# Both FFNs of a decoder layer: gate and up products by Strassen's scheme over pairs of 272-token chunks, with the down products as a stage of their own

## The chip, the cores and the metric

The kernel runs on one core of a Trainium2 chip. The metric is the device time of one execution in microseconds (us). Engines are named as the profile names them: PE is TensorE's matmuls, PEld its weight loads, DVE VectorE, ACT ScalarE, POOL GpSimd, SP SyncE, whose queue issues all the transfers here.

## What is computed

One layer of a hybrid decoder, for 1024 prompt tokens and 64 sample tokens together (1088 columns), in float32:

```
x = x + 1/2 * SwiGLU_1(rmsnorm(x))
z = rmsnorm(x) @ w_in          # attention, recurrent branch, memory, gates
x = x + (sum_b gate_b * (y_b @ W_b_o)) @ w_out
x = x + 1/2 * SwiGLU_2(rmsnorm(x));  y = rmsnorm(x)
swiglu(x) = (silu(x @ w_gate) * (x @ w_up)) @ w_down
```

The model width is 1024 (8 row tiles of 128), the FFN width 2816 (22 tiles of 128, KF). Only the two SwiGLUs, what stands at their seams, and the preparation of weights change.

## The kernel before

Activations are feature-major: 128 features by tokens. The tokens are cut into three chunks of 352, 368 and 368 (CH). A product in float32 is done as three float32r matmuls of 128x128 weights by one chunk (mac3, lines 179 to 181): high weights by high data, high by low, low by high. Each matmul loads its weights anew. So every weight and every activation stands as two parts, a rounded high part that ACT copies and a low part that DVE subtracts.

Weights come by a plan (make_plan), in units of up to 128x1024: SP loads one into one of three raw buffers (line 141), ACT makes its high part (line 153) and DVE its low part (line 154), in one of four split buffers. ahead() makes the next unit while the current one is used.

In ffn() a gate tile and its up tile (144 matmuls: 2 products, 3 chunks, 8 row tiles, 3 matmuls each) are followed by evac: DVE multiplies gate by the reciprocal root-mean-square rbc (line 318), ACT applies Silu (319), DVE takes up times rbc and 1/2 (320), POOL multiplies (321), ACT and DVE split the result h (323, 324), which stays in SBUF. Between them stand the down products of the h tiles that are done: groups of 2, 2, 3, 3, 3, 3, 3 and 3 row tiles (DOWN), one PSUM bank per output tile and chunk, each added into x by DVE (line 348). In the last group, as each x tile becomes final, after() squares it on ACT (236), sums on POOL (238), and splits it for the next stage (198, 199).

```
[(0, 2, 512), (2, 2, 512)] + [(k, 3, 256) for k in range(4, 19, 3)] + [(19, 3, 1024)]
```

x stays in SBUF through an FFN. It is stored after FFN 1 (line 1333) and loaded again for the output projection (out_proj, line 1200), which adds to it, squares and splits it. The order on PE, ACT, DVE and POOL is that of the program's text, which tick() and later() interleave with side work (for instance bias_rows, lines 399 and 400, in FFN 1); SP issues in the program's order as buffers come free. PSUM has six banks for products and two for the rest.

## Time and profile before

| | us |
|---|---|
| runs of the kernel before | 2854.25, 2859.75, 2857.37 |
| median | 2857.37 |
| the profiled execution's own time | 2854.25 |
| its span, first to last instruction | 2854.3 |

The profile gives each engine's busy time over the span, by stretch, and by line. A matmul's own duration overlaps the next one's, so the cost of one in a full stream is the stretch's length over its number of matmuls. FFN 1 runs from 0 to about 818 us, the mixing part to about 1959, the output projection to about 2059, FFN 2 to 2839, and the final norm's tail to the end.

### The profile page before, as it was taken

The page shows a single profiled execution, that of the slowest core. Times are in us where ns is not written, and L with a number is a line of the kernel's source. Part 1 is how long each engine was busy: PE and PEld are TensorE (multiplying, and loading weights), DVE is VectorE, ACT ScalarE, POOL GpSimd, SP SyncE. Part 2 cuts the span into 40 slices and gives each one's busy share as a digit, 9 for nine tenths or more (in the row PEclk, how much of TensorE's full clock was granted, in tenths as well). Part 3 has the DMA queues.
Part 4 walks back from the last instruction along what each step waited for, and adds up shares of the span by engine and source line. Part 5 has one row for each costly group of instructions (what it writes and reads, how often), then busy time and mean ns, then how long its engine had stood idle before and what let it go on. Part 6 is the DMA issues. An engine that isn't in the chain of part 4 may idle for free. (4 is left out here: it accounts for less than half of the span.)

```text
span 2854.3 us, 40939 instructions
## 1 busy us (share of the span) xinstructions
PE 2801.9 (98%) x16762; PEld 2685.4 (94%) x16762; DVE 1309.6 (46%) x2204; ACT 748.5 (26%) x1306; POOL 449.0 (16%) x504
## 2 busy tenths in 40 slices
...
GB/s 155 78 96 72 84 76 62 84 77 62 77 167 120 97 128 71 186 194 183 169 154 147 120 79 56 255 189 191 89 74 74 67 78 78 67 78 78 67 74 63
DMA packets 142107, 308.03 MB, mean 108 GB/s; under 512 B 17800, under 2 KB 95816, under 8 KB 141248
## 3 DMA queue, kind: packets, MB, share of 16 engines
...
## 5 line engine op out<-in xcount | busy, mean ns | idle before, releaser
L179 PE MATMUL pg<-xg,ws 128*128 128x368 f32 (+1 forms) x2112 | 696.4, 330 | 6.1 <-ACT ws L153 6.1
L181 PE MATMUL pg<-xg,ws 128*128 128x368 f32 (+1 forms) x2112 | 694.4, 329 | 2.0 <-DVE ws L154 2.0
L180 PE MATMUL pg<-xg,ws 128*128 128x368 f32 (+1 forms) x2112 | 690.2, 327 | 0.5 <-DVE xg L199 0.5
L179 PE MATMUL z<-xg,ws 128*128 128x368 f32 (+1 forms) x1392 | 479.4, 344 | 6.0 <-DVE ta L1092 6.0
L181 PE MATMUL z<-xg,ws 128*128 128x368 f32 (+1 forms) x1392 | 457.0, 328 | 0.0
L180 PE MATMUL z<-xg,ws 128*128 128x368 f32 (+1 forms) x1392 | 456.1, 328 | 0.0
L154 DVE TENSOR_TENSOR ws<-wr,ws 128x1024 fp32r<-128x1024 f32 (+2 forms) x257 | 306.8, 1195 | 235.4 <-ACT ws L153 235.2
L179 PEld LDWEIGHTS pg<-xg,ws 128*128 128x128 f32 x2112 | 398.8, 189 | 6.4 <-ACT ws L153 6.1
L181 PEld LDWEIGHTS pg<-xg,ws 128*128 128x128 f32 x2112 | 398.9, 189 | 2.7 <-DVE ws L154 2.7
L180 PEld LDWEIGHTS pg<-xg,ws 128*128 128x128 f32 x2112 | 398.7, 189 | 2.4 <-DVE xg L199 2.4
L153 ACT ACTIVATE ws<-wr 128x1024 fp32r<-128x1024 f32 (+2 forms) x257 | 253.6, 989 | 543.6 <-PE pd L181 373.7
L180 PE MATMUL pd<-h,ws 128*128 128x368 f32 (+1 forms) x1056 | 346.2, 328 | 0.0
L179 PE MATMUL pd<-h,ws 128*128 128x368 f32 (+1 forms) x1056 | 346.0, 328 | 0.0
L181 PE MATMUL pd<-h,ws 128*128 128x368 f32 (+1 forms) x1056 | 345.5, 327 | 0.0
L321 POOL TENSOR_TENSOR td<-sl,tb 128x352 f32<-128x352 f32 (+1 forms) x132 | 128.4, 973 | 1336.7 <-DVE tb L320 1302.9
L179 PEld LDWEIGHTS z<-xg,ws 128*128 128x128 f32 x1392 | 263.2, 189 | 28.2 <-issue 19.0
L348 DVE TENSOR_TENSOR x<-x,pd 128x368 f32<-128x368 f32 (+1 forms) x384 | 199.0, 530 | 189.6 <-PE pd L181 189.5
L180 PEld LDWEIGHTS z<-xg,ws 128*128 128x128 f32 x1392 | 263.4, 189 | 2.8 <-issue 0.3
L181 PEld LDWEIGHTS z<-xg,ws 128*128 128x128 f32 x1392 | 262.8, 189 | 0.0
L320 DVE SCALAR_TENSOR_TENSOR tb<-pg,rbc 128x352 f32<-128x352 f32 (+1 forms) x132 | 70.7, 535 | 316.9 <-PE pg L181 316.9
L179 PEld LDWEIGHTS pd<-h,ws 128*128 128x128 f32 x1056 | 198.3, 188 | 0.0
L181 PEld LDWEIGHTS pd<-h,ws 128*128 128x128 f32 x1056 | 198.3, 188 | 0.0
...
## 6 DMA issues: line engine op xcount, KB each, us to landing
...
```

The source lines that it names most:

```text
L153: nc.scalar.activation(spl[:, 0, e], raw[:, e], AF.Copy)
L154: nc.vector.tensor_tensor(out=spl[:, 1, e], in0=raw[:, e], in1=spl[:, 0, e].bitcast(F32), op=OP.subtract)
L179: nc.tensor.matmul(out, wh, xh, start=i == 0, stop=False)
L180: nc.tensor.matmul(out, wh, xl, start=False, stop=False)
L181: nc.tensor.matmul(out, wl, xh, start=False, stop=i == n - 1)
L320: nc.vector.scalar_tensor_tensor(tb, pu[:, :n], 0.5, self.rbc[:, t0:t0 + n], op0=OP.mult, op1=OP.mult)
L321: nc.gpsimd.tensor_tensor(out=td, in0=sl, in1=tb, op=OP.mult)
L348: nc.vector.tensor_tensor(out=xa, in0=xa, in1=ps[:, :n], op=OP.add)
```

## The change

- Gate and up products of all 22 tiles come first, and the down products form a stage after them. h is stored to DRAM as it is made (line 491) and read back for the down stage (hidden, lines 548 to 553), where it is halved and split. The down groups become eleven of 2 row tiles.
- The tokens of gate and up are cut into two pairs (tp) of chunks of 272. Three tiles are done plainly (plain). The other 19 use Strassen's scheme in Winograd's form (quad): rows of weights in two halves, gate and up as the two halves of columns, two token chunks; seven products of 4 row tiles per pair where eight would stand, each with a combination of weights (combined, lines 172 to 205) and a combination of token blocks (token_blocks, sums_of_blocks). Three of the products add onto the banks of others, so a pair takes four banks, and the eight banks go to the two pairs.
- The tokens are scaled by the norm's gains, not by rbc, before they are split. rbc comes in at the evictions (swiglu, plain).
- The last two tiles (ALONE) are done for one token pair, then for the other, each with weights prepared anew, so that the first pair's memory is given to the down stage.
- Weights are split in halves of 512 in seven buffers (RING), with four raw buffers. The three lines of mac3 become 261 to 263.
- x is loaded again for each down stage, from the input in FFN 1, from DRAM in FFN 2 (line 1734). The output projection does chunks 2 and 1, then chunk 0; FFN 2 begins with the second token pair. The bias rows of FFN 1 come later and wait 20 ticks instead of 2.

**DVE in one tile of gate and up.** Before: the evacuation of one chunk (ta, tb, h: gate, up, the low part of h) and the split of a unit of weights (ws from wr). pg is a PSUM bank.

```order
L318 TENSOR_TENSOR ta_1271<-pg_1216,rbc 128x368
L320 SCALAR_TENSOR_TENSOR tb_1272<-pg_1241,rbc 128x368
L324 TENSOR_TENSOR h_1079<-td_1274,h_1079 128x368
L154 TENSOR_TENSOR ws_1301<-wr_1096,ws_1301 128x1024
```

Now, from a Strassen tile of FFN 1: ws is the low part of an operand, s and wr (L182) are the sums of weights, mu, uu and sl the sums of products of the two token pairs.

```order
L167 TENSOR_TENSOR ws_2908<-wr_2594,ws_2908 128x512
L182 TENSOR_TENSOR wr_2594<-wr_2594 128x512
L182 TENSOR_TENSOR s_2872<-wr_2594,wr_2592 128x512
L518 TENSOR_TENSOR uu_2914<-pg_2895,mu_2842 128x272
L518 TENSOR_TENSOR uu_2929<-pg_2916,mu_2857 128x272
L167 TENSOR_TENSOR ws_2944<-s_2872,ws_2944 128x512
L518 TENSOR_TENSOR uu_2914<-pg_2931,uu_2914 128x272
L518 TENSOR_TENSOR uu_2929<-pg_2948,uu_2929 128x272
L167 TENSOR_TENSOR ws_2974<-wr_2594,ws_2974 128x512
L533 TENSOR_TENSOR sl_2977<-pg_2826,rbc 128x272
L533 TENSOR_TENSOR sl_2991<-pg_2844,rbc 128x272
```

Between two operands' low parts there now stand two evacuations, which wait for PE's products of the operand before.

**SP where FFN 2 goes from gate and up to down.** Before, x was loaded once between the merge and the output projection, among the weights of w_out (xs_d is its copy in DRAM, wr a raw weight buffer):

```order
L141 DMA wr_17009<-in_w_out_dram 128x1024
L1200 DMA x_16988<-xs_d_86 128x8x368
L141 DMA wr_17041<-in_w_out_dram 128x1024
L1200 DMA x_16988<-xs_d_84 128x8x352
L141 DMA wr_17075<-in_w_out_dram 128x1024
```

Now it is loaded behind the last store of h (sl is h's buffer; hr a read of h):

```order
L491 DMA h_d<-sl_24824 128x544
L153 DMA wr_24940<-in_w_dn_dram 128x1024
L153 DMA wr_24978<-in_w_dn_dram 128x1024
L153 DMA wr_25034<-in_w_dn_dram 128x1024
L153 DMA wr_25138<-in_w_dn_dram 128x1024
L491 DMA h_d<-sl_24961 128x544
L1734 DMA x_25020<-x_d_82 128x8x352
L1734 DMA x_25020<-x_d_82 128x8x368 x2
L548 DMA hr_25229<-h_d 128x1088
```

The load of x moved from ahead of the output projection to behind the last gate and up tile of FFN 2, and it is in SBUF where that tile's buffers were.

The diff, cut to its core:

```diff
...
+TILES = [*range(KF), *range(KF - ALONE, KF)]
+DOWN = [(k, 2, 512) for k in range(0, KF - 2, 2)] + [(KF - 2, 2, 1024)]
+RING = 7
...
 UNITS = [(2, 0), (2, 1), (1, 0), (1, 1), (0, 0), (0, 1)]
-# tiles of the gates between the parts of the mixing layer: after the memory heads, after the attention heads,
...
...
-            pair = lambda p: [col(gu, p), col(gu, KF + p)]
-            plan, off = pair(0) + pair(1), 0
-            for g, (k, nk, w) in enumerate(DOWN):
-                if w == D:
-                    return plan + [flat(dn, off + j * 128 * D, D) for j in range(nk)]
-                k1, n1, _ = DOWN[g + 1]
-                plan += pair(k1) + [flat(dn, off + j * 128 * nk * w, nk * w) for j in range(D // w)]
-                plan += [u for p in range(k1 + 1, k1 + n1) for u in pair(p)]
+            plan, off = [], 0
+            for n, p in enumerate(TILES):
+                plan += [(gu if n < PLAIN else "*" + gu, i[gu][q], 1024) for q in (p, KF + p)]
+            for k, nk, w in DOWN:
+                n = D if w == D else nk * w
+                plan += [flat(dn, off + j * 128 * n, n) for j in range(nk * D // n)]
                 off += 128 * nk * D
+            return plan
...
-            spl = self.wspl.tile([128, 2, 1024], F32R, name=self.uid("ws"), tag="wspl")
-            for j in range(cuts):
-                e = slice(j * n // cuts, (j + 1) * n // cuts)
-                nc.scalar.activation(spl[:, 0, e], raw[:, e], AF.Copy)
-                nc.vector.tensor_tensor(out=spl[:, 1, e], in0=raw[:, e], in1=spl[:, 0, e].bitcast(F32), op=OP.subtract)
...
+    def part(self, src):
+        nc = self.nc
+        n = src.shape[1]
+        spl = self.wspl.tile([128, 2, 512], F32R, name=self.uid("ws"), tag="wspl")
+        nc.scalar.activation(spl[:, 0, :n], src, AF.Copy)
+        nc.vector.tensor_tensor(out=spl[:, 1, :n], in0=src, in1=spl[:, 0, :n].bitcast(F32), op=OP.subtract)
+        return spl
+    def halves(self, name, raw, n):
+        for a in range(0, n, 512):
+            self.ready.append((name, n, self.part(raw[:, a:min(a + 512, n)])))
+            yield
+    def combined(self, name, g, u):
+        nc = self.nc
+        a11, a12, a21, a22 = g[:, :512], g[:, 512:], u[:, :512], u[:, 512:]
+        s2 = self.sums.tile([128, 512], F32, name=self.uid("s2"), tag="s2", bufs=2)
+        def tt(eng, out, x, y, op):
+            eng.tensor_tensor(out=out, in0=x, in1=y, op=op)
+        def put(m, src):
...
+        put(4, a22)
+        tt(nc.vector, a22, a21, a22, OP.add)
+        tt(nc.vector, s2, a22, a11, OP.subtract)
+        tt(nc.gpsimd, a21, a11, a21, OP.subtract)
+        yield
+        put(6, s2)
+        yield
+        put(7, a21)
+        yield
+        put(5, a22)
+        yield
+        put(2, a12)
+        tt(nc.gpsimd, a12, a12, s2, OP.subtract)
+        yield
+        put(3, a12)
...
+    def make(self):
+        for _ in self.rest:
+            return
+        if self.raws or self.plan:
+            name, raw, n = self.raw()
+            if name[0] == "*":
+                self.rest = self.combined(name, raw, self.raw()[1])
+            else:
+                self.rest = self.halves(name, raw, n)
+            next(self.rest)
+            while len(self.raws) < 2 and self.plan:
+                self.load()
 
     def ahead(self):
-        if len(self.ready) + self.using < 4:
-            self.split()
+        for _ in range(2):
+            if len(self.ready) + self.using < RING:
+                self.make()
...
+    def operand(self, name, m):
+        while True:
+            for x in self.ready:
+                if x[:2] == (name, m):
+                    self.ready.remove(x)
+                    self.using += 1
...
-            nc.tensor.matmul(out, wl, xh, start=False, stop=i == n - 1)
+            nc.tensor.matmul(out, wh, xh, start=start and i == 0, stop=False, **more)
+            nc.tensor.matmul(out, wh, xl, start=False, stop=False, **more)
+            nc.tensor.matmul(out, wl, xh, start=False, stop=i == n - 1, **more)
             if i == min(3, n - 1):
                 self.ahead()
...
+        if gains is None:
+            nc.scalar.activation(t[:, 0], src, AF.Copy)
+            nc.vector.tensor_tensor(out=t[:, 1], in0=src, in1=t[:, 0].bitcast(F32), op=OP.subtract)
...
+        def squares(i, j):
+            src = self.block(xs, i, j)
+            for k in (0, 2):
+                t = pool.tile([128, 2, TC], F32, name=self.uid("sq"), tag="uu", bufs=3)
+                nc.scalar.activation(t, src[:, k:k + 2], AF.Square)
+                for e in range(2):
+                    if j not in acc:
+                        acc[j] = pool.tile([128, TC], F32, name=self.uid("acc"), tag="mu", bufs=2)
+                        nc.gpsimd.tensor_tensor(out=acc[j], in0=t[:, 0], in1=t[:, 1], op=OP.add)
+                        break
+                    nc.gpsimd.tensor_tensor(out=acc[j], in0=acc[j], in1=t[:, e], op=OP.add)
...
+            squares(i, j)
+            for k in range(4):
+                nc.scalar.activation(src[:, k], src[:, k], AF.Copy, scale=self.vec[:, g + 4 * i + k:g + 4 * i + k + 1])
+            if not (quick and n < 2):
+                self.put(tp, m, src)
+            if (1 - i, j) in order[:n]:
+                self.later(3, lambda j=j: rstd(j))
+            yield
...
+        b11, b12, b21, b22 = (self.block(xs, i, j) for i in range(2) for j in range(2))
+        def less(out, x, y):
+            eng.tensor_tensor(out=out, in0=x, in1=y, op=OP.subtract)
+        less(b11, b12, b11)
+        less(b12, b22, b12)
+        less(b22, b22, b11)
+        yield
+        self.put(tp, 6, b22)
+        yield
+        self.put(tp, 7, b12)
+        less(b21, b21, b22)
+        yield
+        while not rest():
+            yield
+        self.put(tp, 5, b11)
+        yield
+        self.put(tp, 4, b21)
+        yield
...
+                for w in ws:
+                    while not all(m in xo for m in ms):
+                        self.tick()
+                    ps = self.mm_bank("pg")
+                    self.mac3(ps[:, :TC], [(w(k, 0), (xo[ms[k // 4]][:, 0, k % 4, :], xo[ms[k // 4]][:, 1, k % 4, :]))
+                                           for k in range(KD)])
+                    both.append(ps)
...
+                def evac(j=j, rb=rb, both=both, sl=sl, uu=uu, tp=tp):
+                    for t, ps in zip((sl, uu), both):
+                        nc.vector.tensor_tensor(out=t[:, j], in0=ps[:, :TC], in1=rb, op=OP.mult)
+                    if j:
+                        self.gated_hidden(p, tp, sl, uu)
+                self.held.append(((tp, j), evac))
+                self.evacuate(2)
+        for _ in ws:
+            self.done()
...
+    def gated_hidden(self, p, tp, sl, uu):
+        nc = self.nc
+        nc.scalar.activation(sl, sl, AF.Silu)
+        nc.gpsimd.tensor_tensor(out=sl, in0=sl, in1=uu, op=OP.mult)
+        nc.sync.dma_start(self.h_d[p, :, tp * TH:(tp + 1) * TH], sl.rearrange("p j n -> p (j n)"))
+    def quad(self, gu, p, tps, pool):
+        banks, steps = {}, {tp: self.swiglu(p, tp, pool) for tp in tps}
+        for m in OPS:
+            w = self.operand("*" + gu, m)
+            for tp in tps:
+                bank = {2: 1, 4: 7, 3: 5}.get(m, m)
+                if bank == m:
+                    banks[tp, m] = self.mm_bank("pg")
+                ps, xo = banks[tp, bank][:, :TC], self.xo[tp][m]
+                self.mac3(ps, [(tuple(w[:, s, k * 128:(k + 1) * 128] for s in range(2)), (xo[:, 0, k, :], xo[:, 1, k, :]))
+                               for k in range(4)], start=bank == m)
+                steps[tp](m, ps)
+            self.using -= 1
...
+        def step(m, ps):
+            if m == 1:
+                new("mu", [TC], 2)
+                nc.scalar.activation(t["mu"], ps, AF.Copy)
+            if m == 6:
+                plus(t["mu"], ps, t["mu"])
+            if m == 7:
+                new("uu", [2, TC], 3)
+                plus(t["uu"][:, 1], ps, t["mu"])
+            if m == 5:
+                plus(t["uu"][:, 1], ps, t["uu"][:, 1])
+            if m == 2:
+                new("sl", [2, TC], 3)
+                nc.vector.tensor_tensor(out=t["sl"][:, 0], in0=ps, in1=rb[:, 0], op=OP.mult)
+            if m == 4:
+                plus(t["uu"][:, 0], ps, t["mu"])
+                nc.gpsimd.tensor_tensor(out=t["uu"], in0=t["uu"], in1=rb, op=OP.mult)
+            if m == 3:
+                sl = t["sl"]
+                plus(sl[:, 1], ps, t["mu"])
+                nc.gpsimd.tensor_tensor(out=sl[:, 1], in0=sl[:, 1], in1=rb[:, 1], op=OP.mult)
+                self.gated_hidden(p, tp, sl, t["uu"])
+        return step
+    def hidden(self, k, pool, raws, wait):
+        nc = self.nc
+        raw = raws()
+        nc.sync.dma_start(raw, self.h_d[k])
+        def split():
+            h = pool.tile([128, 2, NT], F32R, name=self.uid("h"), tag="h", bufs=4)
+            nc.scalar.activation(h[:, 0, :], raw, AF.Copy, scale=0.5)
+            nc.vector.scalar_tensor_tensor(h[:, 1, :], raw, 0.5, h[:, 0, :].bitcast(F32), op0=OP.mult, op1=OP.subtract)
+            self.h[k] = h
+        self.later(wait, split)
...
+        second = 1 - first
+        for p in range(PLAIN):
+            self.copies(copies)
+            self.plain(gu, p, (first, second), pool)
+        self.evacuate(0)
+        self.plained = True
+        while self.first or self.due:
+            self.tick()
+        self.hurry = False
+        for p in range(PLAIN, KF - ALONE):
+            self.copies(copies)
+            misc(p)
+            self.quad(gu, p, (first, second), pool)
+        for tp in (first, second):
+            for p in range(KF - ALONE, KF):
+                self.quad(gu, p, (tp,), pool)
+            if tp == first:
+                change()
...
+    def down(self, dn, pool, raws, after):
+        for g, (k, nk, w) in enumerate(DOWN):
+            ks = range(k, k + nk)
+            if 0 < g < len(DOWN) - 1:
+                for j in range(2):
+                    self.hidden(DOWN[g + 1][0] + j, pool, raws, 8 + 4 * j)
+            if w == D:
+                units = [self.unit(dn, w) for _ in ks]
                 for c in range(3):
-                    evac(p, c, *[product(w, c, 2) for w in ws])
-
-        def down_tile(ks, part, o, c):
-            t0, n = CH[c]
-            ps = self.mm_bank("pd")
-            self.mac3(ps[:, :n], [(part(j), tuple(h[k][:, s, t0:t0 + n] for s in range(2))) for j, k in enumerate(ks)])
-            xa = self.x[:, o, t0:t0 + n]
-            nc.vector.tensor_tensor(out=xa, in0=xa, in1=ps[:, :n], op=OP.add)
-            self.tick()
-
...
             nc.sync.dma_start(self.bias_d[g], row)
             for h in range(4):
...
+        nc = self.nc
+        for tp in (1, 0):
+            nc.sync.dma_start(xs[tp], self.x_d[0][:, :, tp * TH:(tp + 1) * TH])
+        for cs in ((2, 1), (0,)):
...
+                            xa = xs[tp][:, f, a - tp * TH:e - tp * TH]
+                            nc.vector.tensor_tensor(out=xa, in0=xa, in1=ps[:, a - t0:e - t0], op=OP.add)
+                    self.tick()
                 self.done()
-                if 0 in cs:
-                    split(2, f)
-                    if f == 2:
-                        self.norm_chunk(2, accs[2], 2)
-        for c in range(2):
-            for f in range(KD):
-                split(c, f)
-            self.later(2 + c, lambda c=c: self.norm_chunk(c, accs[c], 3))
-
...
+    def change2():
+        low2.close()
+        pools.append(right(low2, "ring2"))
+        four = stage0.tile([128, 4, NT], F32, name="hr4", tag="xs")
+        raws = iter([four[:, k] for k in range(4)])
+        K.first_hidden(pools[-1], lambda: next(raws), lambda: None)
...
-        K.ring = es.enter_context(tc.tile_pool(name="ring2", bufs=4, reuse_waits="tile"))
-        K.tmps = es.enter_context(tc.tile_pool(name="tmps4", bufs=2, reuse_waits="tile"))
+        K.banks(es, "psum6", mm=6, t=2)
...
-        K.out_proj(pool)
+        for t0, n in CH:
+            nc.sync.dma_start(K.x[:, :, t0:t0 + n], K.x_d[1][:, :, t0:t0 + n])
         acc = {}
...
-        K.ffn("w_gu2", "w_dn2", (2, 0, 1), lambda c: None, after2, lambda p: K.copies(1 if p < 21 else 100))
+        K.down("w_dn2", ring, K.raw_tiles(pool), after2)
...
```

## Rows read from the trace of the kernel before

**Rows 1.** The page, part 1: span and busy time by engine.
```profile
span 2854.3 us, 40939 instructions
...
PE 2801.9 (98%) x16762; PEld 2685.4 (94%) x16762; DVE 1309.6 (46%) x2204; ACT 748.5 (26%) x1306; POOL 449.0 (16%) x504
```
**Rows 2.** Busy time by stretch (us, then busy and instructions by engine, clock, DMA share, GB/s): steady FFN.
```profile
2200.00:2300.00 100.00, 100.00 (x609) 100.00 (x608) 38.25 (x65) 16.48 (x27) 8.76 (x9) 1.00 0.22 74
```
**Rows 3.** The page, part 5: one of the gate and up products' three lines.
```profile
L179 PE MATMUL pg<-xg,ws 128*128 128x368 f32 (+1 forms) x2112 | 696.4, 330 | 6.1 <-ACT ws L153 6.1
```
**Rows 4.** Timeline of PE, memory keys (256 columns): the first product, and what follows the last of 96.
```profile
853.15 0.28 PE L179 MATMUL mk<-mg,ws 128*128 128x256 f32 x1
...
864.55 0.39 PE L833 MATMUL mv<-ws,mg 128*128 128x512 f32 x1
864.78 0.39 PE L834 MATMUL mv<-ws,mg 128*128 128x512 f32 x1
```
**Rows 5.** Busy time by stretch: the start, and the bias rows at 140.
```profile
0.00:10.00 10.00, 2.79 (x7) 1.88 (x7) 5.18 (x7) 6.44 (x12) 5.61 (x10) 1.00 0.80 274
10.00:20.00 10.00, 8.61 (x33) 6.90 (x34) 10.00 (x10) 8.84 (x18) 9.69 (x9) 1.00 1.05 393
20.00:30.00 10.00, 10.00 (x65) 10.00 (x64) 10.00 (x16) 6.15 (x13) 1.63 (x2) 1.00 0.16 62
30.00:40.00 10.00, 7.27 (x37) 6.76 (x36) 8.23 (x21) 3.62 (x8) 2.42 (x2) 0.83 0.37 117
140.00:150.00 10.00, 7.16 (x45) 6.87 (x43) 2.52 (x4) 1.97 (x3) 0.98 (x1) 1.00 0.23 75
150.00:160.00 10.00, 9.28 (x44) 8.50 (x45) 2.71 (x6) 1.00 (x2) 0.95 (x1) 0.83 0.60 187
```
**Rows 6.** Groups by form (busy us, mean ns, then idle before): splits and evacuations.
```profile
L154 DVE TENSOR_TENSOR ws<-wr,ws 128x1024 fp32r<-128x1024 f32 x183 | 230.1, 1258 | 180.9 <-ACT ws L153 180.7
L153 ACT ACTIVATE ws<-wr 128x1024 fp32r<-128x1024 f32 x183 | 192.4, 1052 | 481.9 <-PE pd L181 373.7 <-PE pg L181 54.3 <-PE z L181 34.4
L348 DVE TENSOR_TENSOR x<-x,pd 128x368 f32<-128x368 f32 x256 | 135.4, 536 | 145.0 <-PE pd L181 145.0
L321 POOL TENSOR_TENSOR td<-sl,tb 128x368 f32<-128x368 f32 x88 | 86.6, 984 | 600.3 <-DVE tb L320 580.6 <-ACT sl L319 19.5
L690 POOL TENSOR_TENSOR qb<-qb,kv 128x1024 f32<-128x1024 f32 x24 | 57.6, 2398 | 235.1 <-DMA qb<-qs_d 151.9 <-DVE s L510 23.8 <-DVE st L538 16.6
L318 DVE TENSOR_TENSOR ta<-pg,rbc 128x368 f32<-128x368 f32 x88 | 47.3, 537 | 49.3 <-PE pg L181 49.2
L319 ACT ACTIVATE sl<-ta 128x368 f32<-128x368 f32 x88 | 45.1, 512 | 175.5 <-DVE ta L318 175.5
```
**Rows 7.** Instructions of tile mg and of L199 (ns min/median/max, first and last start).
```profile
L800 DVE SCALAR_TENSOR_TENSOR mg<-mraw,vec,mg x8: 477/482/486, 824.7 to 836.3; 128x256 fp32r<-128x256 f32 x8
...
L199 DVE SCALAR_TENSOR_TENSOR xg<-x,vec,xg x72: 576/597/1408, 5.1 to 2062.6; 128x368 fp32r<-128x368 f32 x48, 128x352 fp32r<-128x352 f32 x24
```
**Rows 8.** Timelines at the end of FFN 1: POOL, then DVE.
```profile
785.29 8.20 POOL L238 TENSOR_TENSOR acc<-acc,td 128x352 f32<-128x352 f32 x7 [5.14 <-ACT td L236]
...
787.05 0.84 DVE L199 SCALAR_TENSOR_TENSOR xg<-x,vec,xg 128x352 fp32r<-128x352 f32 x1
...
788.24 0.84 DVE L199 SCALAR_TENSOR_TENSOR xg<-x,vec,xg 128x352 fp32r<-128x352 f32 x1
```
**Rows 9.** Timelines of SP and DVE: x is loaded again before the output projection.
```profile
1959.84 0.59 SPq L1200 DMA_DIRECT2D x<-xs_d  x1
1966.61 0.54 DVE L1216 TENSOR_TENSOR x<-x,wo 128x368 f32<-128x368 f32 x1 [5.21 <-DMA x<-xs_d]
```
**Rows 10.** Busy time by stretch: that load; and the tail.
```profile
1965.00:1970.00 5.00, 5.00 (x32) 5.00 (x31) 1.86 (x3) 1.46 (x2) 0.00 (x0) 1.00 1.05 404
2840.00:2854.30 14.30, 2.35 (x15) 1.86 (x15) 7.55 (x13) 0.93 (x2) 4.57 (x5) 0.57 0.51 185
```
**Rows 11.** Timeline of the tail: the last output stores.
```profile
2846.65 3.83 SPq L1239 DMA_DIRECT2D out_y_dram<-x  x4
```

401 lines of the change are left out of this document (245 added, 156 removed).

## The prediction

> **What bounds the kernel now.** The page's busy times come first: TensorE is busy 98% of 2854.3 us, VectorE 46%, GpSimd 16% [rows 1]. So only the number and length of matmuls, or new waits of TensorE, can move the time. The stretches of both FFNs come next: 609 matmuls in 100 us at full clock, with DVE at 38%, ACT 16%, POOL 9% and the DMA at 0.22 [rows 2]. That is 0.1642 us each at a mean of 1088/3 = 362.7 columns; nothing there waits. Each of the three lines of the gate and up products has 2112 matmuls, 6336 together [rows 3], 1040 us of the span. The other rows give prices for what the change puts in.
>
> The profiled execution took 2854.25 us; the median of the runs is 2857.37, so 3.1 us go on top of a sum made against it. A measurement of this kernel can tell some 0.2%, 5.7 us, from no change.
>
> **The gate and up products.** Per FFN three plain tiles keep 576 matmuls (2 products x 4 blocks x 24). The other 19 take 7 products x 2 token pairs x 12 = 168 each, 3192, where the three chunks had 19 x 144. Both FFNs: 7536 matmuls of 272 columns. No row has 272. The nearest are 256 columns, where 96 matmuls take 853.15 to 864.55, 0.1188 each [rows 4], and 0.1642 at 362.7 [rows 2]. These bound the whole at 895 and 1237 us. The line between them gives 0.000426 us per column; carried to 512 it gives 0.228, and the row there shows 0.23 (864.55 to 864.78), so I take the line: 0.1256. The stage takes 946.5 us instead of 1040.4: **-94**. A tile takes 21.1 us instead of 23.6.
>
> **What the other engines do in a Strassen tile** (the first order extract). VectorE has 9 operations of 512 elements with both inputs in SBUF (seven low parts, two sums of weights) and 12 of 272 from PSUM. By rows of 256 (0.48) [rows 7] and 1024 (1.26) [rows 6] one of 512 takes 0.74; by L318 (0.54 at 368) one of 272 takes 0.43: 6.7 + 5.2 = 11.9 us of 21.1. GpSimd has two of 512 at 1.29, four of 544 at 1.36 and two of 272 at 0.78, between L321 and L690 [rows 6]: 9.6. ACT has seven copies at 0.63, two of 272 and two Silus of 544: 6.6. Two h stores and later one read add 1.1 MB per tile to DMAs at 0.22. What can lengthen this is the two engines meeting: where POOL ran seven sums back to back at 1.17, DVE's L199 took 0.84 against 0.58 free, and one pair of operations came every 1.19 us (787.05 to 788.24) [rows 7, 8]. Free, the pair is 0.58 + 0.95 = 1.53, so it overlaps in part; the factor is 0.78. Even at that, 5.2 + 0.78 x (6.7 + 9.6) = 17.9 is under 21.1: **0**, hidden by TensorE, with 3 us of room. Seven operands of lookahead (10 us of TensorE) cover the order of the queues. If the cover is gone, the tile becomes VectorE's (below).
>
> The Trainium skill speaks against this: on the page "SBUF — State Buffer", section "Who interferes with whom", a VectorE instruction with two SBUF inputs and a GpSimd instruction that reads SBUF exclude each other for the whole instruction. By it the pair above would take 1.53, and the row shows 1.19, so the trace bears out a contention but not a whole exclusion. By it VectorE's time in a tile would be 21.5 and the term about +15 instead of 0.
>
> **Last two tiles, one token pair at a time.** Each pass has 84 matmuls, 10.55 us, and still all nine VectorE operations on weights: 6.7 + 2.6 = 9.3 alone, GpSimd 6.1, met as above 2.6 + 0.78 x 12.8 = 12.6. Eight passes, each short of 2.0 us at most, with 10 us of operands ahead at each row of four; copies of h to be read (1088 elements, 1.3 us) come on top. From 0 to 16, I take **+4**, since the lookahead covers most.
>
> **Start.** Before, 142 matmuls ran in the first 40 us, worth 23.3, so 16.7 were lost [rows 5]; and 89 ran in 140 to 160 (14.6 of 20), 5.4 lost to the bias rows, which the change puts off by 20 ticks. Now ACT prepares eight blocks of 272 tokens: two squares of 544 at 0.66, four scalings at 0.43, one copy of 1088 at 1.1, 4.1 us a block by L319 and L153 [rows 6]. With seven weight halves the first token pair is ready near 25 us and the second near 45, while TensorE has some 18 us of work: about 27 lost. 27 - 16.7 - 5.4 = 5: **+6** (0 if the blocks come as fast as chunks did; 14 if GpSimd's sums hold them).
>
> **End of FFN 1.** The last down group has 2 row tiles instead of 3, so TensorE needs 6 x 0.1642 = 0.99 us per output tile, and VectorE's pair 1.19 [rows 8]: 24 x 0.20 = **+5** (2 with free pairs, 12 at L199's 1.41). The other ten groups are safe: 24 additions at 0.53, four halves and two reads of h are 18 us of 23.6. **Mixing:** split weights come in halves, 0.22 us more VectorE time for each of 129 units, and 3.5 units ahead instead of 4; nearly all is beside TensorE: **+1** (-4 by the fourth raw buffer, +10 if a third of the 28 us counts).
>
> **Output projection to FFN 2.** The blocks are squared, scaled, copied and combined by the same ACT that splits weights; only chunks 2 and 1's 16 tiles and then chunk 0's pass (8 x 24 x 0.16 = 31 us) lie beside eight blocks, 33 us: **+5** (1 to 13).
>
> **FFN 2, gate and up to down** (second extract). x no longer stays in SBUF. Its load lies on SP behind the last h store, and its memory is that of the tile stored. After TensorE's last product: addition 0.43, product 0.78, Silu 0.66, product 1.36, then the store's landing. At the end of the program the last store (issued by 2850.5) lands by 2854.3 [rows 10, 11]: below 4 us for a larger piece; I take 3. x takes 6.8 us from issue to first use (1959.84 to 1966.61) [rows 9] and its other two chunks 3.6 us each (1.47 MB at 404 GB/s) [rows 10]. First addition 13 us after the last product, third chunk 20. Six PSUM banks take 6 tiles, the first two chunks let 8 finish: 7.9 us of work. 20.2 - 7.9 = 12.3, and a lower clock after it, as at 30 to 40 us (0.83) [rows 5], makes **+14**. Bounds: 7, if landing is quick and chunks come together; 20, if the h reads crowd in. FFN 1 reads x from the input in time: 0. **Tail:** the last group is shorter by a third with the same final norm: **+2** (0 to 6).
>
> **Sum.** -94 + 6 + 0 + 4 + 5 + 1 + 5 + 14 + 2 = -57: 2797 against the profiled execution, **2800** against the median.
>
> **Rivals.**
> 1. The stalls are mostly hidden: all terms at their low ends, 0 + 0 + 0 + 2 - 4 + 1 + 7 + 0 = 6: 2769. For it: each has some cover; against it: the first FFN already loses 22 us in its start with less to prepare [rows 5].
> 2. Whole exclusion of VectorE and GpSimd, as worked out from the rows' free durations: a tile is 5.2 + 16.3 = 21.5, 38 x 0.4 = +15; a single pass 2.6 + 12.8 = 15.4, 4.9 over, 39 in eight less two lookaheads of 10: +19 instead of +4. 2830. Against it: 1.19 where it wants 1.53 [rows 8]. This is the rule named above.
> 3. Slower: the lookahead collapses. VectorE's queue is in order, and between the low parts stand evacuations that wait for TensorE (first extract). If an operand's low part is behind the evacuations of the product before it, TensorE waits 2 x 0.43 + 0.74 = 1.6 us. Once in each of 38 tiles costs 61, twice 122: 2861 and 2922. It decides from 1.5 us a tile. For it: in the first 20 us DVE is busy 10 of 10 us with ten operations [rows 5], 1.0 us each. Against it: seven operands are far more than one.
> 4. No gain, because a matmul of 272 columns costs what one of 363 does: 1237 instead of 1040, slower by 140 or more. The 0.1188 of rows 4 all but excludes it.
>
> **How the numbers follow.** The forecast, 2783 to 2820, has a chance of 0.60; the stalls bigger together than summed, 2820 to 2840, 0.10; rival 1 0.16; rival 2 0.07; rivals 3 and 4 0.06 and 0.01. The range 2768 to 2832 leaves out part of the third case and rivals 3 and 4, and takes in the bounds by halves. Faster by over 0.2% (below 2851.7) 0.91, the same 0.02, slower 0.07.
>
> **What would show it.** Right: about 795 matmuls per 100 us in the Strassen tiles (0.1256), PE near 100%, DVE near 60%, POOL 45%; some 25 us of PE idle in the first 50; one PE wait of about 12 us for x after FFN 2's last gate tile, its releaser DVE behind a DMA. Wrong: PE waits for ws in every tile (rival 3), DVE operations of 512 near 1.4 us mean (rival 2), or no wait for x.

## The result, and the profile after

The changed kernel takes 2874.19 us (median of 4 runs, 2873.31 to 2875.31) where the kernel before took 2858.56 in the same series: ratio 1.0051, 95% interval 1.0037 to 1.0065. It is slower, by 15.6 us; 2800 with a range of 2768 to 2832 was forecast. The profiled execution has a span of 2871.6 us, 17.3 more than before. One run of the study, e4_xrows, had a granted clock of 0.76 from start to end and took 3303.75 us; it is not used, and e4b_xrows repeats it.

The page of the changed kernel, its first part and two of its groups (busy us, mean ns, idle before):

```profile
span 2871.6 us, 45875 instructions
...
PE 2745.8 (96%) x17980; PEld 2620.9 (91%) x17980; DVE 1699.0 (59%) x2961; ACT 889.3 (31%) x1673; POOL 780.1 (27%) x726
...
L261 PE MATMUL pg<-xo,ws 128*128 128x272 f32 x2512 | 736.2, 293 | 46.9 <-DVE uu L518 18.9 <-ACT xo L372 10.8 <-ACT ws L166 9.4
...
L167 DVE TENSOR_TENSOR ws<-wr,ws 128x512 fp32r<-128x512 f32 x592 | 477.4, 832 | 317.3 <-ACT ws L166 316.7
```

TensorE's matmuls are busy 56 us less than before [rows 1]; the gate and up products wait 46.9 us in one of their three lines where they waited 6.1 [rows 3]. Busy time by stretch (us, then busy and instructions by engine, clock, DMA share, GB/s):

```profile
0.00:50.00 50.00, 30.37 (x181) 28.36 (x181) 17.86 (x32) 38.64 (x72) 27.26 (x34) 0.86 0.46 175
...
200.00:250.00 50.00, 44.63 (x335) 43.59 (x334) 25.83 (x44) 11.75 (x22) 19.67 (x16) 0.93 0.36 129
...
350.00:400.00 50.00, 50.00 (x401) 50.00 (x401) 30.52 (x54) 13.98 (x26) 22.41 (x18) 1.00 0.35 128
...
500.00:550.00 50.00, 43.62 (x300) 42.13 (x298) 32.30 (x53) 20.10 (x34) 22.18 (x17) 0.91 0.72 257
...
2050.00:2100.00 50.00, 46.42 (x326) 45.89 (x327) 26.81 (x46) 27.11 (x44) 24.67 (x20) 0.97 0.61 208
...
2200.00:2250.00 50.00, 50.00 (x403) 50.00 (x402) 31.55 (x53) 15.48 (x30) 23.37 (x19) 1.00 0.57 196
...
2550.00:2600.00 50.00, 33.67 (x194) 31.49 (x194) 25.01 (x42) 11.44 (x19) 8.92 (x7) 0.83 0.53 186
```

A full stretch of Strassen tiles (350, 2200) holds 402 matmuls, 0.1244 us each, at full clock and with VectorE at 61%: the promise of the products is kept. The rest is lost in a few places, and in each the granted clock falls after the wait: 0.83 to 0.97 are means over 50 us, partly at 2.4 and partly at 1.2 GHz. In what follows, a tile's *lost* time is the time from its first matmul to the next tile's, less 0.1244 us for each of its matmuls (0.1642 for down tiles). By stage, after less before:

| stage | forecast | measured |
|---|---|---|
| gate and up products themselves | -94 | -97 |
| FFN 1 start (before: 21.3 lost to 60 us) | +11 | +13 |
| bias rows (before: 7.8 lost at 120 to 160; after: 23.3 in four tiles) | -5 | +15 |
| eight passes of one token pair | +4 | +29 |
| FFN 1, gate and up to down (2.6 lost), and its last group (2.0 lost before, 7.5 after) | +5 | +8 |
| mixing and merge (1140.7 before, 1152.0 after) | +1 | +11 |
| projection (95.8 before, 102.8 after), start of FFN 2 (2.0 lost before, 13.7 after) | +5 | +19 |
| FFN 2, gate and up to down (17.6 lost), and 0.33 us a down group | +14 | +21 |
| last group of FFN 2 (2.1 lost before, 5.8 after) and tail (15.6 before, 18.4 after) | +2 | +7 |
| sum | -57 | +26 |

The measured rows sum to 26 where the span grew by 17.3. Most of the difference is small losses that the kernel before had elsewhere and that are gone: 4.1 us between 160 and 780, 2.0 between 2080 and 2780. Three rows (bias rows, passes, projection with the start of FFN 2) hold 59 of the 83 us by which the rows missed.

### The profile page after: what moved, and what is told of

Read it like the earlier page. It is cut to its first block, busy times and chain, and to the rows that moved or that the text cites. A ratio compares the mean times of both kernels' runs of the same rounds, so it can differ in the third digit from the quotient of the medians.

```text
span 2871.6 us, 45875 instructions
## 1 busy us (share of the span) xinstructions
PE 2745.8 (96%) x17980; PEld 2620.9 (91%) x17980; DVE 1699.0 (59%) x2961; ACT 889.3 (31%) x1673; POOL 780.1 (27%) x726
## 4 chain that ended last, share of the span: by engine, by line
PE 76%; DVE 7%; DMA 6%; POOL 4%; ACT 3%; issue 3%; SPq 0%; DVEq 0%; ACTq 0%; POOLq 0%
PE pg L261 7%; PE pg L263 7%; PE pg L262 7%; PE z L261 7%; PE z L262 6%; PE z L263 6%; PE pd L261 6%; PE pd L262 6%; PE pd L263 6%; DMA wr<-in_w_gu_dram 2%; PE po L263 2%; PE po L262 2%; PE t L1005 2%; PE po L261 2%; DMA out_sv_dram<-in_cache_v_dram 2%
## 5 line engine op out<-in xcount | busy, mean ns | idle before, releaser
L261 PE MATMUL pg<-xo,ws 128*128 128x272 f32 x2512 | 736.2, 293 | 46.9 <-DVE uu L518 18.9
L263 PE MATMUL pg<-xo,ws 128*128 128x272 f32 x2512 | 731.6, 291 | 4.1 <-DVE ws L167 4.1
L262 PE MATMUL pg<-xo,ws 128*128 128x272 f32 x2512 | 732.4, 292 | 2.7 <-DVE xo L373 2.6
L167 DVE TENSOR_TENSOR ws<-wr,ws 128x512 fp32r<-128x512 f32 x592 | 477.4, 832 | 317.3 <-ACT ws L166 316.7
L166 ACT ACTIVATE ws<-wr 128x512 fp32r<-128x512 f32 x592 | 346.0, 613 | 765.1 <-PE pd L263 392.8
L261 PEld LDWEIGHTS pg<-xo,ws 128*128 128x128 f32 x2512 | 481.5, 192 | 52.1 <-DVE uu L518 21.6
L263 PEld LDWEIGHTS pg<-xo,ws 128*128 128x128 f32 x2512 | 481.6, 192 | 4.8 <-DVE ws L167 4.8
L262 PEld LDWEIGHTS pg<-xo,ws 128*128 128x128 f32 x2512 | 481.8, 192 | 3.8 <-DVE xo L373 3.3
L620 DVE TENSOR_TENSOR x<-x,pd 128x352 f32<-128x352 f32 (+1 forms) x528 | 270.6, 529 | 163.7 <-PE pd L263 148.7
L261 PEld LDWEIGHTS z<-xg,ws 128*128 128x128 f32 x1392 | 263.7, 189 | 28.7 <-issue 19.1
L261 PEld LDWEIGHTS pd<-h,ws 128*128 128x128 f32 x1056 | 200.2, 190 | 16.6 <-DVE x L620 16.0
L262 PEld LDWEIGHTS pd<-h,ws 128*128 128x128 f32 x1056 | 200.6, 190 | 0.0
L263 PEld LDWEIGHTS pd<-h,ws 128*128 128x128 f32 x1056 | 200.5, 190 | 0.0
L320 POOL TENSOR_TENSOR acc<-acc,td 128x368 f32<-128x368 f32 (+1 forms) x41 | 43.2, 1054 | 496.7 <-ACT td L318 494.6
```

The costliest lines, as they stand in the source:

```text
L166: nc.scalar.activation(spl[:, 0, :n], src, AF.Copy)
L167: nc.vector.tensor_tensor(out=spl[:, 1, :n], in0=src, in1=spl[:, 0, :n].bitcast(F32), op=OP.subtract)
L261: nc.tensor.matmul(out, wh, xh, start=start and i == 0, stop=False, **more)
L262: nc.tensor.matmul(out, wh, xl, start=False, stop=False, **more)
L263: nc.tensor.matmul(out, wl, xh, start=False, stop=i == n - 1, **more)
L320: eng.tensor_tensor(out=acc[:, :n], in0=acc[:, :n], in1=t, op=OP.add)
```

## The experiments

Each edit is against the changed kernel, with nothing else different, unless it says so. None leaves out a part of the computation. Most kernels ran once; eleven runs of the kernel before in one series spread over 8.9 us, so a difference of 3 or 4 us in a single time proves little, and the small effects are read from the lost time of their tiles.

**Copies ahead of weight loads: e1_copies, e1b_pieces.** SP's own timeline in the changed kernel, where FFN 1 makes its bias rows:

```profile
180.79 0.65 SPq L1498 DMA_DIRECT2D out_sv_dram<-in_cache_v_dram  x1
182.63 2.46 SPq L653 DMA_DIRECT2D skew_d<-bias_d  x4
...
186.42 0.32 SPq L644 DMA_DIRECT2D br<-c_offs_dram  x1
203.94 0.98 SPq L153 DMA_DIRECT2D wr<-in_w_gu_dram  x2
```

After its seventh small transfer SP stands for 17 us before it issues the next weights. The chain of waits of the same kernel names what it waits for:

```profile
180.79 23.08 DMA out_sv_dram<-in_cache_v_dram
203.94 4.54 DMA wr<-in_w_gu_dram
```

In the program's order with its waits, transfers use eight completion counters in turn, so each waits for the landing of the eighth before it; here that is the copy of 1 MB, which takes 23 us (180.79 + 23.08 = 203.87, and the load is issued at 203.94). The kernel before had the same stand of 18 us, behind a copy and seven small transfers:

```profile
124.79 0.66 SPq L1259 DMA_DIRECT2D out_sk_dram<-in_cache_k_dram  x1
...
129.11 0.32 SPq L394 DMA_DIRECT2D br<-c_offs_dram  x1
147.65 0.99 SPq L141 DMA_DIRECT2D wr<-in_w_gu_dram  x2
```

In the changed kernel the DMA is busy at 0.13 between 195 and 205 us:

```profile
195.00:205.00 10.00, 8.91 (x72) 8.69 (x70) 1.75 (x2) 2.41 (x5) 4.91 (x5) 1.00 0.13 51
```

First edit: no copies in tiles 3 to 10, two each from 11 on.

```diff
...
-    K.gate_up("w_gu1", 0, ev, 1, misc1, change1)
+    K.gate_up("w_gu1", 0, ev, lambda p: 1 if p < 3 else 0 if p < 11 else 2, misc1, change1)
```

> FFN 1 issues no cache copy (1 MB, DRAM to DRAM) in its tiles 3 to 10, where the bias rows are made, and two per tile from tile 11 on; nothing else differs from the changed kernel. Theory (a transfer is issued only when the eighth before it has landed; the bias rows' seven small transfers put the next weight load eighth behind a copy of 23 us): the tiles at 148, 195, 246 and 296 us, which lost 4.3, 9.0, 8.5 and 1.5 us, lose under 2 us each, about 21 us in all come back, 2874 becomes about 2853. Rival (the bias rows themselves, TensorE waiting for their DMA as it did before the change for 3.6 us): the losses stay, 2870 or more. Second rival (bandwidth, copies against weight loads): the losses move to the tiles from 11 on, where two copies run in each.

Measured: 2926.96 us. The four bias tiles lost 1.4, 1.4, 1.4 and 1.5, as the theory has it; but three of the next tiles, with two such copies each, lost 23.0, 20.9 and 22.4, as the second rival has it. The stretch of one of them, where TensorE waits for weights that were issued in time:

```profile
360.00:380.00 20.00, 0.96 (x4) 0.96 (x5) 4.65 (x9) 2.08 (x4) 1.78 (x1) 0.62 0.20 78
```

The chain of waits of this run has, for a load behind two copies that were issued at 290.76 and 291.50:

```profile
292.27 41.02 DMA wr<-in_w_gu_dram
```

So a weight load issued behind such a copy also lands behind it: one copy costs 20 us of the load's time, which the lookahead of one tile just covers; two, or one and a late issue, it doesn't. It is not the bytes: FFN 2 has two copies in each tile, at 0.57 of the DMA, and loses nothing. Its copies are of another shape (1 x 16 outer pieces, not 2 x 8). Second edit: the shape.

```diff
-                nb, cut = ((8, 1), (2, 1), (1, 2))[g]
+                nb, cut = ((8, 1), (1, 1), (1, 2))[g]
```

> The eight cache copies of 2 x 8 x 16128 elements (1 MB) are cut by sequence into sixteen of 1 x 16 x 8064 (0.5 MB); one per tile as before. Theory (such a copy runs on two of the sixteen DMA engines, 0.13 of the DMA in the trace, takes 20 to 23 us, and holds the weight loads behind it; a copy with 16 outer pieces goes over all sixteen): weight loads of FFN 1 land within 6 us of their issue, the four tiles with the bias rows lose under 3 us each instead of 4.3, 9.0, 8.5 and 1.5, and about 15 to 20 us come back, 2874 becomes about 2855. Rival (the small transfers of the bias rows themselves, by their number): the losses stay above 15 us in all, 2868 or more.

Measured: 2852.75 us; the four tiles lost 1.4, 1.4, 1.4 and 1.3. The same stretch now:

```profile
195.00:205.00 10.00, 10.00 (x76) 9.04 (x75) 7.02 (x13) 3.43 (x7) 4.50 (x4) 1.00 0.61 214
```

The theory holds. Of the 21 us by which this run is shorter than the median of the changed kernel, 17.8 are in the four tiles (23.3 lost, then 5.5); the rest is not tied to the copies. The Trainium skill has this on its page "DMA: Bandwidth & Descriptors", section "Why a DMA increments its semaphore by 16 and not by 1": the slowest dimension that isn't 1, of source and destination, sets how many of the sixteen engines a transfer uses, the largest number up to sixteen that divides both. A first dimension of 2 gives two engines, 2/16 = 0.125, and the trace shows 0.13.

**The passes of one token pair: e3_defer, e8_chain, e13_best1, e15_nodefer.** Timelines of the first such pass in FFN 1, ACT, then DVE, then PE:

```profile
488.61 0.66 ACT L489 ACTIVATE sl<-sl 128x544 f32<-128x544 f32 x1 [3.92 <-POOL sl L540]
491.45 0.66 ACT L489 ACTIVATE sl<-sl 128x544 f32<-128x544 f32 x1 [2.19 <-POOL sl L540]
492.02 0.61 ACT L166 ACTIVATE ws<-wr 128x512 fp32r<-128x512 f32 x1
492.54 0.38 ACT L523 ACTIVATE mu<-pg 128x272 f32<-128x272 f32 x1
...
492.74 1.96 DVE L167 TENSOR_TENSOR ws<-wr,ws 128x512 fp32r<-128x512 f32 x2 [5.22 <-ACT ws L166]
...
496.41 0.69 DVE L182 TENSOR_TENSOR s<-wr,wr 128x512 f32<-128x512 f32 x1
497.02 0.43 DVE L518 TENSOR_TENSOR uu<-pg,mu 128x272 f32<-128x272 f32 x1
...
497.50 0.39 PE L261 MATMUL pg<-xo,ws 128*128 128x272 f32 x1 [2.76 <-DVE uu L518]
```

ACT stands at the Silu of the tile before, which waits for GpSimd; the first copies for the new tile queue behind it, VectorE's low parts behind those, and the evacuation uu behind them. TensorE adds product 4 (the sixth in order) onto the bank of product 7 (the third), which uu must have read first, and waits. With two token pairs there are 7.5 us between the end of the one and the start of the other; with one there are 3. VectorE's throughput isn't it; it is busy 8.84 us of this pass:

```profile
486.90:502.10 15.20, 12.44 (x86) 12.12 (x85) 8.84 (x15) 5.58 (x10) 7.88 (x7) 0.89 0.34 112
```

Edit of e3_defer:

```diff
-                self.gated_hidden(p, tp, sl, t["uu"])
+                fin = lambda: self.gated_hidden(p, tp, sl, t["uu"])
+                if p == KF - 1 and tp == self.last:
+                    fin()
+                else:
+                    self.later(3, fin)
...
```

> The Silu of a Strassen tile, the product after it and the store of h are put three steps later in the program, behind the first evacuations and weight copies of the next tile; only the very last is not. Theory (in the eight single passes ACT stands 4 to 5 us at a Silu that waits for GpSimd, the next tile's copies and VectorE's evacuations queue behind it, and TensorE waits for a bank that it adds onto): the eight passes lose 8 to 14 us in all instead of 28.7, 2874 becomes about 2855 to 2862. Rival (weights: VectorE, ACT and the ring can't prepare seven operands in 10.5 us): no change in the passes, 2871 to 2877.

Measured: 2874.3. The eight passes lost 19.9 instead of 28.7 us, less than expected, and the bias tiles lost 38 instead of 23 (SP's stores of h come later, ahead of the weight loads). ACT now stood at a copy that waits for GpSimd's last difference of weights, so the next run takes that link out too:

```diff
-        tt(nc.gpsimd, a12, a12, s2, OP.subtract)
+        tt(nc.vector, a12, a12, s2, OP.subtract)
```

> Both links of the chain at the end of a Strassen tile are taken out of it: the Silu and what follows come three steps later, and the last difference of weights (a12 - s2) moves from GpSimd to VectorE. Theory (queues in program order, not throughput: ACT's copy of the next weights waits for GpSimd, which is at the long product by rstd): the eight single passes lose 4 to 10 us in all, against 28.7 in the changed kernel and 19.9 with the later Silu alone. Rival (VectorE's throughput, which gets 0.7 us more of work per pass): they lose 20 us or more. Time: it has the bias-row losses too, 2850 to 2865.

Measured: 2872.75, over the 2850 to 2865 that were expected, since the bias tiles lost 34.9 (38 in e3_defer); the passes lost 16.9 us, not 4 to 10. The first pass of each FFN now loses 0.2, the second 1.2; the last two, with h's first reads split beside them, lose 1.5 to 5.0. One of those:

```profile
521.00:535.20 14.20, 10.98 (x86) 10.55 (x85) 13.15 (x20) 6.70 (x11) 6.07 (x4) 1.00 0.91 317
```

VectorE is busy 13.15 of 14.2 us, so there the rival's throughput is the likely limit. So both hold, the queue's order in the first passes, the work in the last. The other way is to have fewer passes: with one tile alone (ALONE = 1) the four passes lose 3.9 us in e13_best1 and 2.3 in e14_best, both below, and with the queue order of the change, which e15_nodefer puts back, 11.0. A part of that only moves: with a shorter prefetch, the first down group of FFN 1 loses 7.5 us in e14_best instead of the changed kernel's 2.6.

Its edit, against e14_best, takes back the difference on VectorE and the deferred Silu:

```diff
-        tt(nc.vector, a12, a12, s2, OP.subtract)
+        tt(nc.gpsimd, a12, a12, s2, OP.subtract)
...
+                self.gated_hidden(p, tp, sl, t["uu"])
...
```

> e14_best with the Silu and the last difference of weights where the change has them. Theory (the order of the queues costs each pass of a single token pair 2 to 5 us): the four passes lose 9 to 14 us in all where e14_best loses 3 to 5, so it takes 6 to 10 us more. Rival (only a second pass in a row is short of operands, one pass lives on the lookahead): no difference beyond 3 us.

Measured: 2829.99 against 2821.88 of e14_best: 8 us, as expected, 4.9 and 4.8 of the losses in the first pass of each FFN.

**FFN 2's load of x: e4b_xrows.**

```diff
-        for t0, n in CH:
-            nc.sync.dma_start(K.x[:, :, t0:t0 + n], K.x_d[1][:, :, t0:t0 + n])
+        for k in range(0, KD, 2):
+            nc.sync.dma_start(K.x[:, k:k + 2, :], K.x_d[1][:, k:k + 2, :])
```

> The same kernel as e4_xrows, whose run was at a granted clock of 0.76 throughout, which no change of a transfer's order makes: FFN 2's load of x goes by row tiles. Theory: the first down group of FFN 2 loses 9 to 11 us instead of 17.6, 2874 becomes about 2866. Rival (the h store and the memory): the loss stays within 2 us of 17.6.

Measured: 2868.52; the first down group lost 10.0 instead of 17.6. The order of the pieces is 7.6 us of the wait; by the chain of waits the rest is the store of h (2.0 us) and the first piece (5.0 us), which no run took away.

**Start of FFN 2: e5_early.** The chain of waits of the changed kernel has, at the second half of the second token pair prepared:

```profile
2068.77 12.63 DMA x_d<-x2s
```

ACT's next scaling in place waits 3.75 us for that store to land.

```diff
+                if f % 2:
+                    tp = 1 if 2 in cs else 0
+                    nc.sync.dma_start(self.x_d[1][:, f - 1:f + 1, tp * TH:(tp + 1) * TH], xs[tp][:, f - 1:f + 1, :])
-        K.first.append(K.token_blocks(1, xs[1], g, order, ev, store=store(1)))
+        K.first.append(K.token_blocks(1, xs[1], g, order, ev))
...
```

> The copy of x that FFN 2 reads again is stored two row tiles at a time during the output projection, as they become final, instead of a half at a time when the token blocks are prepared. Theory (the blocks are scaled in place, so ACT's scaling waits until the store has read them, 12.6 us at 2069): the output projection and FFN 2's first two tiles, which lost about 7 and 13.7 us, lose 6 to 10 together, 2874 becomes about 2862. Rival (ACT's own work on the blocks, 4 us each, holds TensorE): the loss stays above 17 us, 2870 or more.

Measured: 2864.99 (one run; FFN 1 and the mixing part of it were 5 us shorter by themselves). FFN 2's first two tiles lost 10.5 instead of 13.7, the projection stayed at 102.8: 3 us, not the 12 expected. The store was a link, but the second tile's 7.9 us come from the next, VectorE's sums of blocks ahead of a low part of weights. So the rival's number came out, but not its cause, ACT's work. In the changed kernel these sums run beside GpSimd's sums of other blocks (the last three lines); the first two lines, from the start of FFN 1, show the same VectorE operations with GpSimd idle:

```profile
58.94 0.68 DVE L167 TENSOR_TENSOR ws<-wr,ws 128x512 fp32r<-128x512 f32 x1
...
61.09 1.28 DVE L429 TENSOR_TENSOR xs<-xs 128x1088 f32<-128x1088 f32 x1
...
2097.48 10.47 POOL L429 TENSOR_TENSOR x2s<-x2s 128x1088 f32<-128x1088 f32 x3
...
2101.99 3.62 DVE L429 TENSOR_TENSOR x2s<-x2s 128x1088 f32<-128x1088 f32 x1
2105.53 2.97 DVE L167 TENSOR_TENSOR ws<-wr,ws 128x512 fp32r<-128x512 f32 x1
```

GpSimd's sum takes 2.56 us with VectorE idle (at 70.06) and 3.5 here; VectorE's takes 3.62 instead of 1.28, the low part 2.97 instead of 0.68. TensorE then waits 3.9 us for that low part. No run took these sums apart.

**The start of FFN 1: e9_dscale, e10_start, e11_rstd, e16_dsum.** Four attempts (e11_rstd was meant for the projection), all slower.

The first gives the scaling in place to VectorE.

```diff
-                nc.scalar.activation(src[:, k], src[:, k], AF.Copy, scale=self.vec[:, g + 4 * i + k:g + 4 * i + k + 1])
+                nc.vector.tensor_scalar(src[:, k], src[:, k], self.vec[:, g + 4 * i + k:g + 4 * i + k + 1], None, op0=OP.mult)
```

> The scaling of the token blocks by the norm's gains in place (four operations of 272 per block) moves from ACT to VectorE, in both FFNs. Theory (ACT sets the start: it is busy 38.6 of the first 50 us, and each block takes 4 us of it): FFN 1's first tile loses 16 to 20 us instead of 23.8, FFN 2's first two 9 to 12 instead of 13.7; 2874 becomes about 2866. Rival (GpSimd's sums of squares and the arrival of x set it): the first tile stays above 22.

Measured: 2884.76, 30.2 lost in the first tile and 16.0 in FFN 2's first two, not 9 to 12. VectorE's timeline has the same four operations twice:

```profile
27.75 3.40 DVE L417 TENSOR_SCALAR xs<-xs,vec 128x272 f32<-128x272 f32 x4
...
33.90 1.18 DVE L417 TENSOR_SCALAR xs<-xs,vec 128x272 f32<-128x272 f32 x4
```

Beside GpSimd's sums they take 0.85 us each; at 33.90, where GpSimd is at an operation of 4 columns (L298), 0.30. This is the contention that the forecast allowed for the Strassen tiles, in another place.

The next squares the first two blocks of the first token pair last.

```diff
+        if quick:
+            for q in range(2):
+                self.put(tp, q + 1, self.block(xs, *order[q]), g + 4 * order[q][0])
+                yield
+        done, order = order[:2], order[2:] + order[:2] if quick else order
         for n, (i, j) in enumerate(order):
...
```

> FFN 1's first token pair: the third and fourth block are squared, scaled and copied before the first and second, which TensorE already has, are squared and scaled. Theory (ACT's order sets when TensorE gets the third block: 7 us of squares and scalings of blocks that are already there lie ahead of it): FFN 1's first tile loses 15 to 19 us instead of 23.8; 2874 becomes about 2868. Rival (the evacuations need rstd, which needs the squares; PSUM has eight banks): the loss only moves to the second and third tile, 2872 or more.

Measured: 2886.10. The first tile lost 26.0 and the second 8.6. TensorE had the third block at 19.1 us instead of 25.1, and then stood for what the evacuations need; its waits up to 75 us:

```profile
PE pg L261 <- ACT ws L166: 8.1, 1, 8.1
PE pg L263 <- DVE ws L167: 6.0, 1, 6.0
PE t L305 <- POOL rs L298: 4.3, 2, 3.6
PE t L293 <- POOL acc L397: 3.6, 2, 3.3
```

Then TensorE's sums for rstd later in its order.

```diff
-                self.later(3, lambda j=j: rstd(j))
+                self.later(8, lambda j=j: rstd(j))
```

> The sums over partitions for rstd, which TensorE does, come eight steps after the squares instead of three. Theory (TensorE takes them in program order and stands until GpSimd's last sum is there, 3.3 us and a lower clock after it at 2044 us): the output projection takes 98 us instead of 102.8, 2874 becomes about 2869. Rival (ACT's splits of weights are late there, behind the token blocks): no change in the projection, 2872 or more.

Measured: 2906.05. The projection took 99.9 us instead of 102.8, where 98 was expected, but FFN 1's first tile lost 39.3 and FFN 2's first two 20.8 instead of 13.7: a later sum is a later rstd, and the evacuations wait for it. TensorE's longest wait in FFN 1's start is 15.9 us for rstd from GpSimd (rs, L298). e16_dsum moves the sums of squares to VectorE on top of e10's order and of e14_best:

```diff
-        acc = {}
+        acc, sums = {}, nc.vector if quick else nc.gpsimd
...
-                        nc.gpsimd.tensor_tensor(out=acc[j], in0=t[:, 0], in1=t[:, 1], op=OP.add)
+                        sums.tensor_tensor(out=acc[j], in0=t[:, 0], in1=t[:, 1], op=OP.add)
```

> e14_best with FFN 1's third and fourth block first, and the sums of squares of the first token pair on VectorE instead of GpSimd. Theory (both must be early: the blocks for the products, the sums for rstd, on which the evacuations and then the banks wait): the first three tiles lose 16 to 21 us instead of 26.7, about 7 us less than e14_best. Rival (ACT's total work on eight blocks, 4 us each, sets it whatever the order): the three tiles lose 25 or more.

Measured: 2838.30; 35.0 lost in the first three tiles against 27.1 in e14_best. The theory fell, and the rival's number came out, but its cause isn't shown: ACT is busy 39.6 us of the first 50 here and 38.7 in e14_best, nearly the same work, and 8 us more are lost. TensorE's waits are those of e10_start (6.0 for a low part, 4.2 for GpSimd's rs, 3.3 for a sum), so moving the sums took none of them away. What sets the 27 us stays open.

**The mixing part: e19_mem.** Of the 11 us, 8 lie ahead of the first product of the memory keys, which comes 45.3 us after the part's first product instead of 37.2. SP's timeline of the changed kernel, where the memory tokens are loaded; TensorE later waits 4.2 us for their sum of squares:

```profile
818.58 1.55 SPq L153 DMA_DIRECT2D wr<-in_w_mem_kv_dram  x2
820.35 0.38 SPq L856 DMA_DIRECT2D cmask<-c_cmask_dram  x1
...
821.28 0.43 SPq L1041 DMA_DIRECT2D mraw<-in_mem_dram  x1
```

Of before, the same load is ahead of the mask and the weights:

```profile
817.43 0.45 SPq L791 DMA_DIRECT2D mraw<-in_mem_dram  x1
821.11 0.37 SPq L606 DMA_DIRECT2D cmask<-c_cmask_dram  x1
```

The edit, against e14_best, puts the memory tokens' pool on the other side, where nothing lies that is still in use:

```diff
-            with tc.tile_pool(name="memg", bufs=1, reuse_waits="tile") as mpg:
+            with tc.tile_pool(name="memg", bufs=1, side="right", reuse_waits="tile") as mpg:
```

> e14_best with the buffers of the memory tokens on the other side of SBUF, away from x of FFN 1. Theory (the load of the memory tokens waits for the landing of the last store of x, whose memory it takes, and TensorE then waits for their sum of squares): the load is issued 4 us earlier, the first 40 us of the mixing part take 4 to 6 us less, 2822 becomes about 2817. Rival (ACT and VectorE, busy with the last chunk's splits, are what comes late): less than 2 us.

Measured: 2824.75 (median of 4), the same as e14_best. The load was still issued 8 us after the part's first product: its own memory was not what it waited for. It stands behind two weight loads, for which SP waits 3.8 us until VectorE has read a raw buffer, and two masks. That SP's order is the cause is read from these rows; moving the load ahead was not tried.

**All together: e12_best, e13_best1, e14_best.**

e12_best has the edits of e1b_pieces, e4b_xrows, e5_early, e8_chain, e10_start and e11_rstd.

> All edits together: copies over sixteen engines, FFN 2's x by row tiles, the early stores of x, the later Silu and product with the last difference on VectorE, the third and fourth block first, the sums for rstd later. If the terms add up: -21 (copies) - 8 (x) - 4 (stores) - 12 (passes) - 6 (start) - 5 (rstd) from 2874, about 2818, 1.4% under the kernel before. If a rest of the loss is only moved: 2830 to 2845.

Measured: 2852.11 (8 runs), ratio to the kernel before 0.9977 (0.9966 to 0.9987), slower than either figure expected: the start lost 41.0 in its first two tiles, where the changed kernel lost 24.4.

e13_best1 adds one tile alone instead of two:

```diff
-PLAIN, ALONE = 3, 2
+PLAIN, ALONE = 3, 1
```

> The same with one tile instead of two done for one token pair at a time. Theory of the passes (each loses 2 to 5 us to the order of the queues and VectorE's work, whatever their number): four passes fewer give back 8 us, but the down stages have a shorter prefetch: h's first four reads and x in FFN 1 come in one pass of 10.5 us less; up to 8 us lost there. 2806 to 2822.

Measured: 2842.88 (4 runs), ratio 0.9945 (0.9927 to 0.9962); 9 us came back, but the start still lost 41.0, and 2806 to 2822 was missed. The passes lost 3.9 instead of e12_best's 17.7, FFN 1's first down group 7.2 instead of 1.1.

e14_best is e13_best1 without the edits of e10_start and e11_rstd.

> e13_best1 without its two edits on rstd and the order of the first blocks: copies over sixteen engines, x by row tiles, early stores of x, later Silu and last difference on VectorE, one tile alone. If the terms add up: from e13_best1's 2843, 35.0 + 6.0 fall to 24 + 3 at the start (-14) and FFN 2's start from 9.6 + 8.5 to 2.5 + 7.9, with the projection 2.8 us longer (-5): about 2824, 1.2% under the kernel before. If the terms hide each other: 2835 or more.

Measured: 2821.88 (4 runs), ratio to the kernel before 0.9872, interval 0.9855 to 0.9888. It is 52 us faster than the changed kernel and 1.3% faster than the one before. Its lost time has fallen in the four bias tiles from 23.3 to 4.4 us, in the passes from 28.7 to 2.3, in FFN 2's first two tiles from 13.7 to 10.5 and in its first down group from 17.6 to 11.2; in FFN 1's first down group it has risen from 2.6 to 7.5. These sum to 50 of the 52 us. It has 17980 matmuls as the changed kernel has:

```profile
span 2817.9 us, 45846 instructions
...
PE 2729.0 (97%) x17980; PEld 2609.0 (93%) x17980; DVE 1719.5 (61%) x2983; ACT 887.9 (32%) x1659; POOL 739.9 (26%) x682
```

## Why the prediction was wrong

The sum failed at three of its terms: the bias rows (-5, measured +15), the passes of one token pair (+4, measured +29), and the projection with the start of FFN 2 (+5, measured +19). Each put waits at nothing or nearly nothing that the runs and traces then showed. The term of the products was right.

- **The products** were right: 0.1244 to 0.1253 us at 272 columns where the line between two rows gave 0.1256, and 21.0 us a tile. With VectorE at 12.6 of 21.0 us and GpSimd at 10.0, against 11.9 and 9.6 forecast, the Strassen tiles lose nothing: rival 2 fell there. The Trainium skill's rule of exclusion ("SBUF — State Buffer", "Who interferes with whom") isn't decided by that tile: the 21.5 of the prediction let VectorE stand for all of GpSimd's time, but by the rule only those of its operations meet GpSimd's that have two inputs in SBUF, and the twelve evacuations have one in PSUM. Where the engines do meet, at the start of FFN 2 (2097.20 to 2108.50), VectorE's four operations and GpSimd's three took 11.3 us together, and one engine at a time they take 4.5 and 7.7: nearly a whole exclusion there, and dearer than the 0.78 that the prediction took from its rows.
- **The bias rows** are the step that failed first: "5.4 lost to the bias rows, which the change puts off by 20 ticks" counted them as gone. They lost 23.3 us, 17.8 of them by the copies. The rows that told of it stood there before the change too: 3.6 us of TensorE's wait for the same small load, 7.8 us lost at 120 to 160, and on SP the stand of 18 us above. The price was read as TensorE's wait, and not followed back to what the load was behind. And "two h stores and later one read add 1.1 MB per tile to DMAs at 0.22" reasoned with the mean share: 0.22 hides a copy that holds two engines for 23 us.
- **The passes of one pair**: "since the lookahead covers most" looked at weights and at VectorE's throughput. What was late was an evacuation that TensorE needs itself, because products add onto banks in use; cutting the time between the two from 7.5 to 3 us made the chain through ACT, GpSimd and VectorE visible. Of 28.7 us some 17 remain with the chain cut, and 2.3 with half the passes and the chain cut, at the price of 5 us in FFN 1's first down group.
- **Projection to FFN 2**: +5 was ACT's work against TensorE's, and it measured +19; missing were the in-place scaling behind a store (3 us shown) and TensorE's own sums for rstd in program order (3 us in e11_rstd's projection, which its later rstd cost again elsewhere). The other 13 us no run took away; 7.9 of them are the second tile, where the trace shows VectorE's sums of blocks and a low part of weights slowed beside GpSimd's sums. The prediction priced the meeting of the two engines for the Strassen tiles and not here.
- **FFN 2, gate and up to down**: the right wait, at 17.6 for 12.3 plus a lower clock, and with the cause that was given.
- **The start** was near: +13 for +11. Of the 142 matmuls that the prediction counted to 40 us only 123 are gate and up products (the others are small ones of the norm, and a few that two stretches share), so 19.8 us were lost there before, not 16.7. Likewise 157 of the 181 now in the first 50 us are products, and 30 us were lost there where 27 were forecast. The edits tried made it longer, and what sets it is open.
- **The ends**: the last group of FFN 1 measured +5.5 for +5, and 2.6 us were lost ahead of it at gate and up to down, put at 0; the last group of FFN 2 with the tail measured +7 for +2, which no run looked into.
- **The mixing part**: one number, +1, for a change of SP's order that had not been looked at there. It measured +11; its cause is not shown.

Rival 3, a collapsing lookahead once or twice per tile, was the right kind of mechanism in the wrong place: VectorE's queue in program order did decide, in the passes of one pair and not in the 38 tiles. The sign was wrong since four terms that were put at 5 us or less measured 11 to 29.
